# Narrow first row blocks in the products of quarters of a two-layer decoder

## The chip, the cores and the metric

The kernel runs on one core of a Trainium2 chip. The metric is the device time of one execution in microseconds (us); the time before is the median of three runs. The profile is one execution taken by the hardware profiler; its times are counted from the first instruction of the span.

Engine names: PE is TensorE (PEld its weight loads, which overlap the matmuls), DVE is VectorE, ACT is ScalarE, POOL is GpSimd, SP is SyncE, which here issues most DMAs. L1073 is line 1073 of the kernel.

## The reference

256 tokens of width 2048 pass through two layers, each a token mixer and a feed-forward part. Layer 0 mixes with forgetting attention, layer 1 with a mixture of dilated windows. The change lies in the feed-forward part:

```python
def rms_norm(x, g):
    xf = x.astype(jnp.float32)
    y = xf * lax.rsqrt(jnp.mean(xf * xf, axis=-1, keepdims=True) + EPS)
    return (y * g.astype(jnp.float32)).astype(x.dtype)

def sq_relu_mlp(h, w_up, w_down):
    a = jax.nn.relu(h @ w_up)
    return (a * a) @ w_down

for i in range(DEPTH):                      # DEPTH = 2
    h = rms_norm(x, mix_norm_g[i])
    ...                                     # mix: fox_attention or dilated_attention
    x = x + mix
    h = rms_norm(x, mlp_norm_g[i])
    x = x + sq_relu_mlp(h, mlp_w_up[i], mlp_w_down[i])
```

`w_up` is 2048 x 8192 and `w_down` 8192 x 2048, all in float32.

## The kernel before

**Products.** A float32 operand is split into a rounded high part and a residue, and a product is three matmuls: high by high, high by residue, residue by high. Weights stream from HBM in tiles of 256 rows by 512 columns (`raw`, five buffers, 512 KB each). ScalarE casts a tile to its high part (`wh`), VectorE subtracts to get the residue (`wl`); both have five buffers. `split` does this for one unit and is called each time TensorE has used one up, so the feeders run up to five units ahead of TensorE. An ordinary unit (a row block) takes twelve matmuls of 512 columns (L437 to L439).

**Products of quarters.** Of the feed-forward's up product, ten of sixteen column tiles in each layer, twenty in all, are computed with seven products of blocks in place of eight (a Strassen-like scheme, `SEVEN`): the 256 tokens are halved and the 256 x 512 weight tile is cut into four quarters of 128 rows by 256 columns. TensorE multiplies sums of the token halves (`sumT`, made once per layer) or the halves themselves (`hT`) with sums of quarters or the quarters themselves. Per weight tile two units come out of the feeders: `quarters` (three quarters of the tile as they are, 768 columns) and `sums` (four sums that VectorE forms in `sum_quarters`, 1024 columns). `slice_steps` then issues one slice: seven products of three matmuls. The slices are woven between the row blocks of other products at places listed by hand (`BETWEEN` and its sisters), eight slices for one column tile, so that a product of quarters has eight slices (`pr` 0 to 7) some 5 us apart. `halves_chain` afterwards combines the seven results on ScalarE and VectorE (L1038 to L1048).

**PSUM.** The seven results of a product, 128 x 256 each, lie in four banks of 512 columns: `SEVEN` lists for each its bank, the half of the bank, the weight quarter or sum, and the token operand:

```python
SEVEN = ((0, 0, 2, 5), (1, 0, 0, 4), (2, 0, 1, 0), (3, 0, 7, 6), (0, 1, 5, 3), (1, 1, 6, 2), (2, 1, 4, 1))
```

The first four products write the first halves of the four banks, the last three the second halves of banks 0 to 2. In the first slice of a product (`pr == 0`), the first matmul of each of products 0 to 2 streams 512 columns: its own weight quarter and, behind it, a quarter of zeros, which GpSimd writes into the free fourth quarter of that unit's `wh` (unit kind `"first quarters"`, L368). So the start of the accumulation group covers the whole bank, and the bank's second product only accumulates. All other matmuls of a slice stream 256 columns.

**Order.** The order of each engine's instructions is that of the trace of the Python program (`pin`). GpSimd's queue holds the zeroing, a few small vector operations and the accumulating DMAs that add the down product to the residual stream (`add_chain`, L945).

Of the kernel before, what the change touches and what calls it, by code (L numbers as in the profile page):

```python
# [9 lines left out]
F32 = mybir.dt.float32  # L10
# [11 lines left out]
NC = 512  # L22
NX = D // NC
KC = D // P
# [19 lines left out]
HC = NC // 2  # L44
# [61 lines left out]
def trunk(ctx: ExitStack, tc, x, fox_w_in, fox_b_f, fox_q_gain, fox_k_gain, fox_w_out, dil_w_in,  # L106
          dil_q_gain, dil_k_gain, dil_w_out, mix_norm_g, mlp_norm_g, mlp_w_up, mlp_w_down, out):
    nc = tc.nc
# [142 lines left out]
    plan = []  # L251

    units = []
    woven = {"count": 0, "due": {}, "do": None}

    def add(w, rows, cols):

        for r in range(rows[0], rows[1], RAW_SUB * P):
            units.append((len(plan), "rows"))
            plan.append((w, r, cols))  # L260
            for at in woven["due"].get(woven["count"], ()):
                units.extend(((len(plan), "quarters" if at[1] else "first quarters"), (len(plan), "sums")))
                plan.append(at)
            woven["count"] += 1

    def add_group(*chunks, parts=PARTS):

        for a, b in parts:
            for w, cols in chunks:
                add(w, (a * P, b * P), cols)  # L270

    def add_out(w):
        add_group(*((w, [(n * NC, NC)]) for n in range(3)), parts=OUT_PARTS)
        for n in range(3, NX):
            add(w, (0, D), [(n * NC, NC)])

    for j in range(4):
        for part in range(3):
            add(fox_w_in[0], (0, D), [(part * D + j * NC, NC)])
# [66 lines left out]
    def split(parts=(slice(0, W_SUB),)):  # L346
        i = state["split"]
        if i >= len(units):
            return
        hi = wpool.tile([P, W_SUB, NC], F32R, tag="wh", name=f"wh{i}", bufs=W_BUFS)  # L350
        lo = wpool.tile([P, W_SUB, NC], F32R, tag="wl", name=f"wl{i}", bufs=W_BUFS)
        splits.append((hi, lo))
        state["split"] += 1
        for part in parts:
            split_part(i, part)
        if parts:
            next_load()

    def split_part(i, part):
        nonlocal summing  # L360
        n, of = units[i]
        raw, (hi, lo) = raws[n], splits[i]
        if of == "sums":
            raw = quarters.pop()
        if "quarters" in of:

            if of == "first quarters":
                nc.gpsimd.memset(hi[:, 1, HC:NC].bitcast(F32), 0.0)  # L368
            flat_hi, flat_lo, flat = (x.rearrange("p k n -> p (k n)")[:, 0:3 * HC] for x in (hi, lo, raw))
            nc.scalar.copy(flat_hi, flat)  # L370
            for _ in summing or sum_quarters(n):
                pass
            summing = None
            nc.vector.tensor_sub(flat_lo, flat, flat_hi.bitcast(F32))  # L374
            return
        nc.scalar.copy(hi[:, part, :], raw[:, part, :])  # L376

        coming = i + 1 < len(units) and "quarters" in units[i + 1][1]
        if coming:
            summing = sum_quarters(units[i + 1][0])  # L380
            next(summing)
        nc.vector.tensor_sub(lo[:, part, :], raw[:, part, :], hi[:, part, :].bitcast(F32))  # L382
        if coming:
            next(summing)

    quarters, summing = [], None

    def sum_quarters(n):


        raw = raws[n]
        t = work.tile([P, 2, NC], F32, tag="sd", name=f"quarters{n}", bufs=1)
        neg, c, d = t[:, 0, HC:NC], t[:, 1, 0:HC], t[:, 1, HC:NC]
        nc.vector.tensor_sub(t[:, 0, :].rearrange("p (q n) -> p q n", q=2),
                             raw.rearrange("p k n -> p (k n)")[:, HC:3 * HC].rearrange("p (q n) -> p q n", q=2),
                             raw[:, 1, HC:NC].unsqueeze(1).to_broadcast([P, 2, HC]))
        yield
        nc.vector.tensor_add(c, raw[:, 0, HC:NC], neg)
        yield
        nc.vector.tensor_sub(d, raw[:, 0, 0:HC], c)  # L400
        quarters.append(t)
# [11 lines left out]
    def in_turn(w, apart=NC // 2):  # L413
        return w.rearrange("p (b h n) -> p b n h", n=apart, h=2)
# [644 lines left out]
    def slice_steps(tag, banks, pr):  # L1059

        (bh, bl), (th, tl) = splits[used[0]:used[0] + 2]
        for i, (bank, half, w, a) in enumerate(SEVEN):
            hi, lo = (in_turn((t if w > 3 else x)[:, w % 4 // 2, HC * (w % 2):HC * (w % 2) + HC], HC // 2)[:, 0]
                      for x, t in ((bh, th), (bl, tl)))
            if a < 4:
                ah, al = (x[:, a, :] for x in sumT[tag, pr])
            else:
                ah, al = (hT[tag][pr][:, a % 2, x, (a - 4) // 2 * P:((a - 4) // 2 + 1) * P] for x in range(2))
            to = banks[bank][:, HC * half:HC * half + HC]
            if pr == 0 and i < 3:  # L1070

                wide = bh.rearrange("p k (q n) -> p (k q) n", q=2)[:, w:4:3 - w]
                nc.tensor.matmul(banks[bank], ah, wide.rearrange("p b (h n) -> p b n h", h=2), start=True, stop=False)  # L1073
            else:
                nc.tensor.matmul(to, ah, hi, start=pr == 0 and i == 3, stop=False)  # L1075
            nc.tensor.matmul(to, ah, lo, start=False, stop=False)  # L1076
            nc.tensor.matmul(to, al, hi, start=False, stop=pr == KC // 2 - 1 and i > 2)  # L1077
            if i == 2 or i == 6:
                used[0] += 1
                split()  # L1080
                jobs.tick()

    def mlp(tag, **after):
# [3 lines left out]
        def one(b, n, pr):  # L1087
            if pr == 0:
                banks[:] = [pool.tile([P, NC], F32, tag=of, name=f"halves_{tag}_{b}_{n}_{i}")
                            for pool, of in ((ps_tp, "tp"), (ps_sc, "sc")) for i in range(2)]  # L1090
            jobs.need(("sums", tag, pr))
            slice_steps(tag, banks, pr)
            if pr == KC // 2 - 1:
                jobs.spawn(halves_chain(list(banks), f"{tag}a{b}", n, aTs[b], (tag, "free", b - 1, n),
                                        (tag, "halves") if (b, n) == (3, 3) else None))
# [28 lines left out]
    def normed(tag, col, wait=lambda n: 2, later=lambda n: 2):  # L1124
        ssp = norm_begin(tag)
        return lambda n: norm_chain(tag, col, n, ssp, wait(n), later(n))


    first = normed("n0", 0, lambda n: (0, 3, 5, 9)[n], lambda n: (13, 12, 9, 7)[n])
# [24 lines left out]
    row_blocks = [slice(i, i + 1) for i in range(W_SUB)]  # L1154
    split(())
    split_part(0, row_blocks[0])
    jobs.spawn(first(0))
    split_part(0, row_blocks[1])
    next_load()
    split(())  # L1160
# [85 lines left out]
```

## Time and profile before

| | |
|---|---|
| median of three runs | 2104.18 us (2104.1 to 2104.22) |
| profiled execution, first to last instruction | 2099.8 us, the only time given of it; the runs' median is 4.4 us more |
| TensorE (PE) busy | 2094.2 us, 11515 matmuls |
| VectorE (DVE) busy | 1775.9 us |
| ScalarE (ACT) busy | 1299.5 us |
| GpSimd (POOL) busy | 141.3 us |
| DMA | 518.28 MB, mean 247 GB/s |
| matmuls of the wide opening form (L1073) | 60 |
| GpSimd's zeroing (L368) | 20, 0.311 us each |

A row of the timeline gives the start in us, the duration in us, the engine, the line, the operation, the tile written and the tiles read, the shapes, and in brackets the idle time before it with what ended it. The recorded duration of a matmul includes the way through the array and overlaps the next matmul, so its cost in a stream is the distance between two starts. The waits name the waiting engine and line, what it waited for, the sum in us, the number of times and the longest. The chain is followed back from the last instruction; its pieces give a start, a length and an engine with its line.

### The profile page before, as it was taken

To read this page: it belongs to the slowest core of one execution; us is meant where nothing else is said; L and a number is where in the kernel's file an instruction comes from. 1 tells how busy PE (TensorE), PEld (TensorE's weight loads), DVE (VectorE), ACT (ScalarE), POOL (GpSimd) and SP (SyncE) were. 2 spreads that over 40 slices of the span, in tenths; PEclk is the share of its full clock that TensorE was granted. 3 is DMA by queue.
4 is the path that set the end of the run, shared out by engine and by line. 5 is a ranking of instruction groups with operands and counts; after the bars stand their busy time and mean duration, and the time that the engine had idled before them with its cause. 6 is when DMAs were issued, how large, how long until landed. Compare 5 with 4: busy or idle time off the path is not lost.

```text
span 2099.8 us, 32579 instructions
## 1 busy us (share of the span) xinstructions
PE 2094.2 (100%) x11515; PEld 1881.5 (90%) x11515; DVE 1775.9 (85%) x2613; ACT 1299.5 (62%) x1895; POOL 141.3 (7%) x162
## 2 busy tenths in 40 slices
PE   9999999999999999999999999999999999999999
PEld 7888888899999999998888888888899999999998
DVE  6888876989999999998768787767899989999974
ACT  6565654766666666664655665646656766666663
POOL 2000000001100100110010010000001101001000
PEclk9999999999999999999999999999999999999999
DMA  8888877887888877887877776867878878788884
GB/s 258 254 264 262 259 248 222 272 261 241 252 243 249 262 240 252 258 249 236 280 239 230 247 242 211 269 202 243 277 231 261 241 250 248 231 251 256 265 262 152
DMA packets 375010, 518.28 MB, mean 247 GB/s; under 512 B 43112, under 2 KB 176576, under 8 KB 374848
## 3 DMA queue, kind: packets, MB, share of 16 engines
q1 hardware_dynamic: 360608, 503.23, 75.4%
q0 software_dynamic: 13824, 12.59, 4.0%
q8 instruction: 90, 1.47, 0.3%
q14 instruction: 72, 0.59, 0.1%
q10 hardware_dynamic: 416, 0.39, 0.1%
HBM read 463.12 MB, written 40.39 MB: 240 GB/s over the span
## 4 chain that ended last, share of the span: by engine, by line
PE 100%; DVE 0%; ACT 0%; issue 0%
PE acc L437 26%; PE acc L438 26%; PE acc L439 26%; PE halves_n L1077 6%; PE halves_n L1076 6%; PE halves_n L1075 6%; PE halves_n L1073 1%; PE sc_d L749 0%; PE sc_f L749 0%; PE po_f L698 0%; PE po_d L698 0%; PE sc_d L746 0%; PE acc L486 0%; PE acc L485 0%; PE acc L487 0%; PE pf L760 0%
## 5 line engine op out<-in xcount | busy, mean ns | idle before, releaser
L382 DVE TENSOR_TENSOR wl<-raw,wh 128x1024 fp32r<-128x1024 f32 (+1 forms) x643 | 775.6, 1214 | 228.0 <-ACT wh L376 217.9
L376 ACT CAST wh<-raw 128x1024 fp32r<-128x1024 f32 (+1 forms) x643 | 664.9, 1043 | 403.7 <-PE acc L439 323.7
L437 PE MATMUL acc<-wh,hT_n 128*128 128x512 f32 x1280 | 486.5, 380 | 0.4 <-ACT hT_n L580 0.3
L438 PE MATMUL acc<-wl,hT_n 128*128 128x512 f32 x1280 | 485.4, 379 | 0.0
L439 PE MATMUL acc<-wh,hT_n 128*128 128x512 f32 x1280 | 485.3, 379 | 0.0
L376 ACT CAST wh<-quarters 128x1024 fp32r<-128x1024 f32 x160 | 168.0, 1050 | 260.8 <-DVE quarters L400 243.4
L439 PEld LDWEIGHTS acc<-wh,hT_n 128*128 128x128 f32 x1280 | 241.9, 189 | 34.6 <-DVE hT_n L581 0.4
L437 PEld LDWEIGHTS acc<-wh,hT_n 128*128 128x128 f32 x1280 | 242.1, 189 | 33.2 <-ACT hT_n L580 1.0
L438 PEld LDWEIGHTS acc<-wl,hT_n 128*128 128x128 f32 x1280 | 242.2, 189 | 32.6 <-DVE wl L382 0.5
L382 DVE TENSOR_TENSOR wl<-quarters,wh 128x1024 fp32r<-128x1024 f32 x160 | 195.1, 1219 | 43.0 <-ACT wh L376 43.0
L437 PE MATMUL acc<-wh,aTh_n1a 128*128 128x512 f32 x512 | 194.3, 379 | 0.0
L438 PE MATMUL acc<-wl,aTh_n1a 128*128 128x512 f32 x512 | 194.0, 379 | 0.0
L439 PE MATMUL acc<-wh,aTl_n1a 128*128 128x512 f32 x512 | 194.0, 379 | 0.0
L438 PE MATMUL acc<-wl,aTh_n3a 128*128 128x512 f32 x480 | 182.2, 380 | 0.0
L437 PE MATMUL acc<-wh,aTh_n3a 128*128 128x512 f32 x480 | 182.1, 379 | 0.0
L439 PE MATMUL acc<-wh,aTl_n3a 128*128 128x512 f32 x480 | 181.9, 379 | 0.0
L1077 PE MATMUL halves_n<-wh,sums_n 128*128 128x256 f32 x640 | 176.0, 275 | 0.0
L1076 PE MATMUL halves_n<-wl,sums_n 128*128 128x256 f32 x640 | 176.0, 275 | 0.0
L1075 PE MATMUL halves_n<-wh,sums_n 128*128 128x256 f32 x620 | 170.5, 275 | 0.0
L374 DVE TENSOR_TENSOR wl<-raw,wh 128x768 fp32r<-128x768 f32 x160 | 152.3, 952 | 0.0
L370 ACT CAST wh<-raw 128x768 fp32r<-128x768 f32 x160 | 133.1, 832 | 28.9 <-PE acc L439 15.1
L1077 PE MATMUL halves_n<-wh,hT_n 128*128 128x256 f32 x480 | 132.0, 275 | 0.0
(660 smaller groups left out, 3499.1 us busy)
## 6 DMA issues: line engine op xcount, KB each, us to landing
raw<-in_mlp_w_up_dram SPq DMA_DIRECT2D x256, 512.0 KB, 5.1
raw<-in_mlp_w_down_dram SPq DMA_DIRECT2D x256, 512.0 KB, 4.9
raw<-in_dil_w_in_dram SPq DMA_DIRECT2D x192, 256.0 KB, 3.5
raw<-in_fox_w_in_dram SPq DMA_DIRECT2D x94, 512.0 KB, 4.8
raw<-in_fox_w_out_dram SPq DMA_DIRECT2D x32, 512.0 KB, 4.9
raw<-in_dil_w_in_dram SPq DMA_DIRECT2D x32, 512.0 KB, 4.4
raw<-in_dil_w_out_dram SPq DMA_DIRECT2D x32, 512.0 KB, 3.6
x<-y_n POOLq DMA_DIRECT2D x96, 128.0 KB, 6.0
```

The costliest lines, as they stand in the source:

```text
L370: nc.scalar.copy(flat_hi, flat)
L374: nc.vector.tensor_sub(flat_lo, flat, flat_hi.bitcast(F32))
L376: nc.scalar.copy(hi[:, part, :], raw[:, part, :])
L382: nc.vector.tensor_sub(lo[:, part, :], raw[:, part, :], hi[:, part, :].bitcast(F32))
L437: nc.tensor.matmul(acc[t], ah[:, tok], hi, start=first, stop=False)
L438: nc.tensor.matmul(acc[t], ah[:, tok], lo, start=False, stop=False)
L439: nc.tensor.matmul(acc[t], al[:, tok], hi, start=False, stop=last)
L1073: nc.tensor.matmul(banks[bank], ah, wide.rearrange("p b (h n) -> p b n h", h=2), start=True, stop=False)
L1075: nc.tensor.matmul(to, ah, hi, start=pr == 0 and i == 3, stop=False)
L1076: nc.tensor.matmul(to, ah, lo, start=False, stop=False)
L1077: nc.tensor.matmul(to, al, hi, start=False, stop=pr == KC // 2 - 1 and i > 2)
```

## The change

The two kinds of first unit become one: GpSimd writes no zeros any more. In every slice all 21 matmuls stream 256 columns. In the first slice the bank's first product (half 0) opens the accumulation group; the first matmul of the bank's second product (half 1) opens none and falls on columns that nothing has been written to since that opening. `skip_group_check` concerns the program's own bookkeeping of groups and no instruction.

```diff
@@ add
             for at in woven["due"].get(woven["count"], ()):
-                units.extend(((len(plan), "quarters" if at[1] else "first quarters"), (len(plan), "sums")))
+                units.extend(((len(plan), "quarters"), (len(plan), "sums")))
                 plan.append(at)
@@ split_part
-        if "quarters" in of:
-
-            if of == "first quarters":
-                nc.gpsimd.memset(hi[:, 1, HC:NC].bitcast(F32), 0.0)
+        if of == "quarters":
             flat_hi, flat_lo, flat = (x.rearrange("p k n -> p (k n)")[:, 0:3 * HC] for x in (hi, lo, raw))
...
-        coming = i + 1 < len(units) and "quarters" in units[i + 1][1]
+        coming = i + 1 < len(units) and units[i + 1][1] == "quarters"
@@ slice_steps
             to = banks[bank][:, HC * half:HC * half + HC]
-            if pr == 0 and i < 3:
-
-                wide = bh.rearrange("p k (q n) -> p (k q) n", q=2)[:, w:4:3 - w]
-                nc.tensor.matmul(banks[bank], ah, wide.rearrange("p b (h n) -> p b n h", h=2), start=True, stop=False)
-            else:
-                nc.tensor.matmul(to, ah, hi, start=pr == 0 and i == 3, stop=False)
-            nc.tensor.matmul(to, ah, lo, start=False, stop=False)
-            nc.tensor.matmul(to, al, hi, start=False, stop=pr == KC // 2 - 1 and i > 2)
+            nc.tensor.matmul(to, ah, hi, start=pr == 0 and not half, stop=False, skip_group_check=True)
+            nc.tensor.matmul(to, ah, lo, start=False, stop=False, skip_group_check=True)
+            nc.tensor.matmul(to, al, hi, start=False, stop=pr == KC // 2 - 1, skip_group_check=True)
```

## The prediction

> **What bounds the kernel now.** I read the page's first and fourth parts, then TensorE's timeline inside the second half of the feed-forward layers, then the waits of the engines that feed TensorE.
>
> ```profile
> PE 2094.2 (100%) x11515; PEld 1881.5 (90%) x11515; DVE 1775.9 (85%) x2613; ACT 1299.5 (62%) x1895; POOL 141.3 (7%) x162
> ...
> PE 100%; DVE 0%; ACT 0%; issue 0%
> ```
>
> and the view of the cores, span and granted clock:
>
> ```profile
> core 0: 2099.8 us, clock 1.000
> ```
>
> TensorE is busy all the time, the chain that ended last runs through it alone, and its granted clock is full. A record of a matmul overlaps the next one, so a full PE row proves little by itself. What decides is the distance from one start to the next. The timeline of the first row block of a product of quarters (a slice of 21 matmuls, the first of its product):
>
> ```profile
> 450.61 0.38 PE L1073 MATMUL halves_n<-wh,hT_n 128*128 128x512 f32 x1
> 450.83 0.27 PE L1076 MATMUL halves_n<-wl,hT_n 128*128 128x256 f32 x1
> 450.94 0.28 PE L1077 MATMUL halves_n<-wh,hT_n 128*128 128x256 f32 x1
> ...
> 451.93 0.28 PE L1075 MATMUL halves_n<-wh,hT_n 128*128 128x256 f32 x1
> 452.04 0.28 PE L1076 MATMUL halves_n<-wl,hT_n 128*128 128x256 f32 x1
> ...
> 453.27 0.38 PE L437 MATMUL acc<-wh,aTh_n1a 128*128 128x512 f32 x1
> ```
>
> and the slice that follows in the same product:
>
> ```profile
> 455.86 0.27 PE L1075 MATMUL halves_n<-wh,hT_n 128*128 128x256 f32 x1
> ...
> 458.20 0.38 PE L437 MATMUL acc<-wh,aTh_n1a 128*128 128x512 f32 x1
> ```
>
> A wide matmul holds TensorE for 0.22 us (450.61 to 450.83), a narrow one for 0.11. The first slice takes 453.27 - 450.61 = 2.66 us, the ordinary one 458.20 - 455.86 = 2.34 us; 2.66 is 3 wide and 18 narrow spacings, 2.34 is 21 narrow ones. So nothing but the streaming of columns sets the time here: TensorE is not waiting for anybody.
>
> **The change part by part.** First, the three wide matmuls of each first slice become narrow.
>
> ```profile
> L1075 PEld LDWEIGHTS halves_n<-wh,sums_n x620: 192/192/192, 452.2 to 2022.6; 128*128 128x128 f32 x155
> ...
> L1073 PE MATMUL halves_n<-wh,hT_n x40: 379/380/454, 450.6 to 1978.5; 128*128 128x512 f32 x40
> ...
> L1073 PE MATMUL halves_n<-wh,sums_n x20: 382/382/402, 451.5 to 1978.9; 128*128 128x512 f32 x20
> ```
>
> These are rows of the view of the tile that the quarters' products write (count, then shortest, median and longest in ns). There are 40 + 20 = 60 of them, three for each of 20 products. The whole slices give the price with the least rounding: 2.66 - 2.34 = 0.32 us, and the single slices read 0.31 to 0.32; I take 0.314, which is 3 x 0.105. Twenty times that is 6.28 us.
>
> What no row of before shows is a matmul that neither accumulates nor starts a group, which the first matmuls of the banks' second products become (three in each first slice). I bound it from the rows on both sides: the accumulating narrow matmul at 0.11 (450.83 to 450.94), and, above, the wide one at 0.22. The nearest row is the fourth product's start at 451.93: it opens a group with 256 columns, so it overwrites, and the next one starts 0.11 later. I take 0.11, no extra cost. Something cheaper than 0.11 is excluded, since the same 256 columns stream in every case. The Trainium skill, "PSUM — Partial Sum Buffer", in its passage on two groups open in one bank, says that a start clears the written marks of the whole bank and that a later product on other columns then overwrites without a start; no run here shows that yet.
>
> The Trainium skill, "TensorE: Matmul & The Clock Gate", section "Back-to-back issue gap", has a rule that speaks against the gain: in a stream of weight load and matmul pairs the two share the spacing, about 81 ns at 128 columns and 131 ns at 512. By a straight line between these, an estimate, 256 columns would take 98 ns and the 60 edits would bring 60 x 0.033 = 2.0 us; the rows above (0.22 and 0.11) disagree, and the sum goes by them.
>
> Second, GpSimd's zeroing goes, 20 times.
>
> ```profile
> L368 POOL MEMSET wh<- x20: 311/311/312, 440.5 to 1969.2; 128x256 f32 x20
> ```
>
> and from the waits of the whole span (engine and line, released by, us in total, times, longest):
>
> ```profile
> POOL x L945 <- ACT y_n L944: 373.0, 23, 36.9
> ```
>
> The first one runs at 440.5, ten microseconds ahead of its slice at 450.61, and GpSimd is 7% busy. Behind it on GpSimd's queue stand the accumulating DMAs of L945, and what these waited for, 23 times and 373 us, is ScalarE's output, not the memset. So nobody gets work earlier: I cost it at nothing, and it needs no cover, as the work goes and isn't moved. The waits for a free bank, which now may stand before up to seven openings of a first slice instead of four, hold up everything behind them on TensorE if they are late; that is priced below.
>
> Third, whether the feeders keep up with a TensorE that is 0.314 us faster in 20 places. The same view of the waits holds this row:
>
> ```profile
> ACT wh L376 <- PE acc L439: 331.2, 240, 2.1
> ```
>
> ScalarE, the first of the two feeders, waited 240 times for TensorE to give a weight buffer back: at those points the feeders are as far ahead as five buffers allow, and a faster TensorE pulls them along. Between them they are on their own, and inside a product they are slower than TensorE. VectorE's timeline, one round of a row block and a slice:
>
> ```profile
> 1747.75 0.69 DVE L394 TENSOR_TENSOR quarters<-raw 128x512 f32<-128x512 f32 x1
> 1748.36 1.22 DVE L382 TENSOR_TENSOR wl<-raw,wh 128x1024 fp32r<-128x1024 f32 x1
> ...
> 1751.56 1.23 DVE L382 TENSOR_TENSOR wl<-quarters,wh 128x1024 fp32r<-128x1024 f32 x1 [0.32 <-ACT wh L376]
> 1752.82 0.69 DVE L394 TENSOR_TENSOR quarters<-raw 128x512 f32<-128x512 f32 x1
> ```
>
> A round takes VectorE 1752.82 - 1747.75 = 5.07 us; TensorE needs twelve wide matmuls (12 x 0.2155 = 2.59) and a slice (2.34), 4.93 us. Each round eats 0.14 us of the lead. The chain between 1700 and 2000 us, its longest pieces, shows where the lead was used up:
>
> ```profile
> 1749.77 0.35 PE acc L438
> 1754.84 0.35 PE acc L438
> 1759.91 0.35 PE acc L438
> 1780.49 0.32 PE halves_n L1073
> 1781.04 0.24 PE halves_n L1073
> 1860.47 0.24 PE acc L438
> ```
>
> Against 0.2155 these matmuls are late by 0.135 three times, then 0.10, 0.02 and 0.02: 0.55 us in all. So in two products of the second layer (the ones whose slices surround 1750 and 1860) VectorE sets the time, and TensorE's 0.314 us become waiting: 2 x 0.31 = 0.62 lost. The other products have room. Of those the tightest is the one ending in the slice at 678.55 (VectorE's row first, then TensorE's, with a slice of the round shown above):
>
> ```profile
> 677.44 1.23 DVE L382 TENSOR_TENSOR wl<-quarters,wh 128x1024 fp32r<-128x1024 f32 x1 [0.32 <-ACT wh L376]
> ```
>
> ```profile
> 678.55 0.27 PE L1075 MATMUL halves_n<-wh,hT_n 128*128 128x256 f32 x1
> ...
> 1752.11 0.27 PE L1075 MATMUL halves_n<-wh,hT_n 128*128 128x256 f32 x1
> ```
>
> The residues written by 678.67 are first read by the slice's eleventh matmul, 678.55 + 10 x 0.111 = 679.66: 0.99 us ahead. In the round without room above, the same operation ends at 1752.79 for a read at 1753.22: 0.43 ahead. The room is 0.56 us, more than the 0.314 that one first slice takes from it, and the buffers refill between products.
>
> The stop at 1780 is of another kind, a bank that the product before has not given back:
>
> ```profile
> 1779.80 0.41 DVE L1045 TENSOR_TENSOR c_n3a<-c_n3a,halves_n 128x256 f32<-128x256 f32 x1
> 1780.25 0.42 DVE L1047 TENSOR_TENSOR c_n3a<-halves_n,c_n3a 128x256 f32<-128x256 f32 x1
> ```
>
> VectorE reads the old sums of a bank until 1780.21 and those of another until 1780.67, and the late pieces at 1780.49 and 1781.04 are the openings of the second and third wide product, some 0.3 us behind these ends. These readers run on VectorE's time, so the second and third openings can't come earlier than now, and only what is saved in the third remains: 0.105 of 0.314, 0.21 lost. The sum: 6.28 - 0.62 - 0.21 = 5.45 us. The span of 2099.8 becomes 2094.3; the runs' median of 2104.18 lies 4.4 us above the span, and nothing of that start and end is touched, so 2104.18 - 5.45 = 2098.7 us.
>
> **The rivals.** (a) The narrow opening isn't shorter: its 0.19 us weight load (the LDWEIGHTS row) sets the spacing, or a start takes the time of the whole bank that it clears. With the load, 60 x (0.2155 - 0.19) = 1.5 us, so 2102.7; with the bank, nothing, 2104.2. For it speaks that loads are as busy as 90% of the span; against it the narrow start at 451.93 with its neighbour 0.11 later, and the ordinary slice, where 21 loads went by in 2.34 us. The shared spacing of the skill's TensorE page would end at about the same place. Chance 0.06.
>
> (b) The feeders take back more. If the room in the five next tightest products were under 0.31 too, 5 x 0.314 = 1.57 us more would be lost: 2100.3, which is no measurable change. For it speaks that VectorE's round is longer than TensorE's everywhere in these products; against it the 0.56 us of room in the tightest one. Chance 0.05.
>
> (c) Slower: a matmul that overwrites unwritten columns without a start lets the matmul before it leave the array. A narrow record lasts 0.275 and its successor starts after 0.11, so emptying costs 0.164 each. For the 60 second openings that is 9.8 us: 2098.7 + 9.8 = 2108.5; if all 120 openings that become narrow did it, 2118. It decides from 0.161 us for each of the 60, since 5.45 + 4.2 must be made up. No row has such a matmul, which leaves it open; against it the 0.11 after the narrow start, an overwrite too. Chance 0.04.
>
> **How the numbers follow.** The measurement can tell about 0.2%, 4.2 us: faster is under 2099.97, slower over 2108.39. My own case has 0.85. Its low end is nothing lost and the present 0.55 us of stops gone as well: 2104.18 - 6.28 - 0.55 = 2097.3. The high end is the lower edge of (b) with the spread of the three runs, 2100.4. This leaves out (a), (c) and a part of (b), so no wider range is called for. Faster 0.85, the same 0.11 from (a) and (b), slower 0.04.
>
> **What would show it.** All matmuls of the quarters have 256 columns, 60 more on the line that holds the first of the three products, and L368's memset is gone from GpSimd. First slices last 2.34 us like the others. The pieces near 1750 and 1860, some 4 us earlier then, are longer by 0.31 us in sum for each of the two products, and the stop at the first slice after the former grows to about 0.33 us. The first layer, ten products, is shorter by 3.1 us with no stop in it. I am wrong if a second opening in a bank is followed by more than 0.11 us, if stops appear in the first layer, or if TensorE waits for banks in other first slices.

## The result, and the profile after

The changed kernel takes 2097.78 us (median of six runs, 2095.8 to 2098.54) against 2104.14 us of before (six runs, 2103.01 to 2105.31). The ratio is 0.9971, 95% interval 0.996 to 0.9982: 6.4 us less by the medians. The forecast was 2098.7, between 2097.3 and 2100.4.

The page of after, its span and the engines' busy times:

```profile
span 2096.7 us, 32543 instructions
...
PE 2089.2 (100%) x11515; PEld 1877.3 (90%) x11515; DVE 1774.4 (85%) x2613; ACT 1296.4 (62%) x1895; POOL 134.8 (6%) x142
```

The count of matmuls is the same, GpSimd has its 20 instructions less, and the span is only 3.1 us shorter. The six runs after list span and time for each execution, and the time is 1.7 us above the span every time. By that distance the profiled execution of before, with its 2099.8, would have taken 2101.5: it was a lucky one, some 2.6 us under its median. (Later runs of the kernel before list both too, with the same 1.7 us.) So a single pair of profiles doesn't show the size of the gain; its parts do.

TensorE's timeline at the first slice of a product, where before had three wide matmuls:

```profile
451.47 0.27 PE L1067 MATMUL halves_n<-wh,hT_n 128*128 128x256 f32 x1
451.58 0.28 PE L1068 MATMUL halves_n<-wl,hT_n 128*128 128x256 f32 x1
...
452.81 0.28 PE L1067 MATMUL halves_n<-wh,sums_n 128*128 128x256 f32 x1
452.92 0.28 PE L1068 MATMUL halves_n<-wl,sums_n 128*128 128x256 f32 x1
...
453.14 0.28 PE L1067 MATMUL halves_n<-wh,sums_n 128*128 128x256 f32 x1
453.25 0.28 PE L1068 MATMUL halves_n<-wl,sums_n 128*128 128x256 f32 x1
...
453.81 0.38 PE L434 MATMUL acc<-wh,aTh_n1a 128*128 128x512 f32 x1
```

The slice takes 453.81 - 451.47 = 2.34 us; before it was 2.66. The row at 451.47 opens a bank with 256 columns, the rows at 452.81 and 453.14 are second products on unwritten columns without a group of their own: each of the three is followed after 0.11 us.

What the feeders take back is seen in TensorE's late starts. Two places of after, the first in VectorE's and TensorE's timelines of the first layer:

```profile
672.44 1.23 DVE L379 TENSOR_TENSOR wl<-quarters,wh 128x1024 fp32r<-128x1024 f32 x1 [0.32 <-ACT wh L373]
```

```profile
672.99 0.27 PE L1067 MATMUL halves_n<-wh,hT_n 128*128 128x256 f32 x1
```

The residues end at 673.67 and are first read at 672.99 + 1.11 = 674.10: 0.43 us ahead, which is no room, in the sixth slice of the product for which the prediction counted 0.99 in the seventh. The second place is the first slice at 1776.8 in the second layer, VectorE's rows and then TensorE's:

```profile
1768.30 1.23 DVE L379 TENSOR_TENSOR wl<-raw,wh 128x1024 fp32r<-128x1024 f32 x1 [1.24 <-ACT wh L373]
...
1778.10 0.41 DVE L1042 TENSOR_TENSOR c_n3a<-c_n3a,halves_n 128x256 f32<-128x256 f32 x1
```

```profile
1777.04 0.28 PE L1069 MATMUL halves_n<-wh,hT_n 128*128 128x256 f32 x1
1778.65 0.35 PE L1067 MATMUL halves_n<-wh,hT_n 128*128 128x256 f32 x1 [1.34 <-DVE c_n3a L1042]
```

TensorE stands for 1.5 us until the product before has been read out of a bank. VectorE reads late; it stood for 1.24 us itself at 1768.30, and ScalarE's row just ahead of that shows what it stood for, a weight tile that landed late:

```profile
1767.22 2.19 ACT L373 CAST wh<-raw 128x1024 fp32r<-128x1024 f32 x2 [1.59 <-DMA raw<-in_mlp_w_down_dram]
```

The same kind of stop, 0.19 us long in all, stands in the first slice at 695.70 in the first layer, VectorE's reads and then the openings some 0.15 us behind their ends:

```profile
695.46 0.41 DVE L1042 TENSOR_TENSOR c_n1a<-c_n1a,halves_n 128x256 f32<-128x256 f32 x1
695.91 0.42 DVE L1044 TENSOR_TENSOR c_n1a<-halves_n,c_n1a 128x256 f32<-128x256 f32 x1
```

```profile
696.03 0.34 PE L1067 MATMUL halves_n<-wh,hT_n 128*128 128x256 f32 x1
...
696.48 0.35 PE L1067 MATMUL halves_n<-wh,sums_n 128*128 128x256 f32 x1
```

The two later profiles of this kernel have it there too, with 0.23 and 0.19 us.

### The profile page after: what moved, and what is told of

It reads as the page before. It is cut to its first block, busy times and chain, and to the rows that moved or that the text cites. A ratio compares the mean times of both kernels' runs of the same rounds, so it can differ in the third digit from the quotient of the medians.

```text
span 2096.7 us, 32543 instructions
## 1 busy us (share of the span) xinstructions
PE 2089.2 (100%) x11515; PEld 1877.3 (90%) x11515; DVE 1774.4 (85%) x2613; ACT 1296.4 (62%) x1895; POOL 134.8 (6%) x142
## 4 chain that ended last, share of the span: by engine, by line
PE 95%; DVE 2%; DMA 1%; issue 1%; ACT 0%; SPq 0%; ACTq 0%; DVEq 0%
PE acc L434 25%; PE acc L435 25%; PE acc L436 25%; PE halves_n L1069 6%; PE halves_n L1068 6%; PE halves_n L1067 6%; DVE wl L379 1%; DMA raw<-in_mlp_w_up_dram 1%; ACT wh L373 0%; PE sc_d L746 0%; DMA x<-in_x_dram 0%; PE sc_f L746 0%; PE po_d L695 0%; PE sc_d L743 0%; PE acc L482 0%
## 5 line engine op out<-in xcount | busy, mean ns | idle before, releaser
L435 PE MATMUL acc<-wl,hT_n 128*128 128x512 f32 x1280 | 485.4, 379 | 0.0
L436 PE MATMUL acc<-wh,hT_n 128*128 128x512 f32 x1280 | 485.3, 379 | 0.0
L1067 PE MATMUL halves_n<-wh,sums_n 128*128 128x256 f32 x640 | 176.2, 275 | 0.0
L1069 PE MATMUL halves_n<-wh,sums_n 128*128 128x256 f32 x640 | 176.0, 275 | 0.0
L942 POOL DMA_DIRECT2D x<-y_n x96 | 84.2, 1357 | 970.3 <-ACT y_n L941 837.1
```

Of the source, the lines that this page charges most:

```text
L435: nc.tensor.matmul(acc[t], ah[:, tok], lo, start=False, stop=False)
L436: nc.tensor.matmul(acc[t], al[:, tok], hi, start=False, stop=last)
L942: nc.gpsimd.dma_start(xt[n][:, t, h * HC:h * HC + HC], y, accum_op=ALU.add)
L1067: nc.tensor.matmul(to, ah, hi, start=pr == 0 and not half, stop=False, skip_group_check=True)
```

## The experiments

All ten were timed beside the kernel before. For each profile I also took, from TensorE's timeline, the distance from the first to the last start of the quarters' matmuls in each layer, and the stops in it (how much later than 0.2155 or 0.111 us after its predecessor a matmul starts, where that is over 0.025). The stretch between the layers' slices is 594.83 or 594.84 us, and the stretch behind the last one 76.8 to 76.9, in all of these profiles but that of the GpSimd sum (77.2 behind); the stretch ahead of the first varies from 450.6 to 452.4 without a pattern.

| kernel | ratio to before (95%) | layer 1: us, stops | layer 2: us, stops |
|---|---|---|---|
| before | 1 | 488.46, 0.00 | 489.01, 0.52 |
| after | 0.9971 (0.996 to 0.9982) | 485.73, 0.40 | 487.79, 2.48 |
| after, in the second group of runs | 0.9976 (0.9965 to 0.9987) | 486.18, 0.84 | 486.55, 1.22 |
| after, in the fourth group | 0.9972 (0.9961 to 0.9983) | 486.54, 1.19 | 486.05, 0.70 |
| zeroing put back | 0.9975 (0.9965 to 0.9985) | 485.55, 0.19 | 487.48, 2.17 |
| narrow in layer 1 only | 0.9987 (0.9978 to 0.9996) | 486.72, 1.40 | 488.82, 0.37 |
| narrow in layer 2 only | 0.9988 (0.9979 to 0.9997) | 489.32, 0.85 | 486.83, 1.51 |
| wide in two slices | 1.0025 (1.0015 to 1.0035) | 491.58, 0.00 | 493.12, 1.53 |
| after, lighter sums | 0.9964 (0.9952 to 0.9977) | 485.33, 0.00 | 485.33, 0.00 |
| before, lighter sums | 0.9993 (0.9984 to 1.0002) | 488.46, 0.00 | 489.08, 0.62 |
| slices spread | 0.9982 (0.9974 to 0.9991) | 487.65, 2.33 | 487.97, 2.65 |
| pause moved | 0.998 (0.9971 to 0.9989) | 486.55, 1.20 | 486.70, 1.36 |
| sums first | 1.0005 (0.9996 to 1.0014) | 488.56, 3.25 | 490.34, 5.03 |
| sum on GpSimd | 1.0473 (1.0459 to 1.0487) | 538.51, 53.32 | 538.56, 53.39 |

Less its stops, every layer comes to 485.2 to 485.4 us where it is narrow, to 488.5 where it is wide and to 491.6 with the wide form in two slices. So the streaming and the stops are all that differs between these layers.

Theory A was that the gain is the streaming of 60 matmuls and that VectorE, with the banks it must read, takes a part back.

**The zeroing put back.** The change without its second part:

```diff
+            if n in firsts:
+                nc.gpsimd.memset(hi[:, 1, HC:NC].bitcast(F32), 0.0)
             nc.scalar.copy(flat_hi, flat)
```

> The changed kernel with GpSimd's 20 zeroings put back (their values are read by nobody now). Theory A, the gain is the narrower streaming of 60 matmuls alone: the time is that of the changed kernel within 0.3%, about 2097.8 us, ratio to before 0.997, and first slices of 2.34 us. Rival B, part of the gain comes from the zeroing that is gone: the time goes back towards before by up to 20 x 0.31 = 6.2 us, to 2104.

2097.56 us, ratio 0.9975: that of the changed kernel. Its GpSimd groups hold the 20 zeroings again:

```profile
L371 POOL MEMSET wh<- 128x256 f32 x20 | 6.2, 312 | 574.0 <-PE halves_n L1074 259.6 <-DVE wl L384 229.6 <-PE acc L441 84.8
```

So their 6.2 us of GpSimd cost nothing that the timed runs, good to some 2 us, or the layers less their stops can tell, and rival B falls.

**Narrow in one layer only.** From the kernel before, with `NARROW` 0 for the first and 1 for the second:

```diff
-            if pr == 0 and i < 3:
+            narrow = tag == ("n1", "n3")[NARROW]
+            if pr == 0 and i < 3 and not narrow:
```

> Narrow openings in the ten products of the first layer only; the second layer as before. Theory A: 30 x 0.105 = 3.1 us saved, less what stops near VectorE's limit take (up to 0.5), so 2101.3 us and the distance from the first to the last slice of layer 1 shorter by 2.7 to 3.1 us, that of layer 2 unchanged. Rival C, the gain is the whole span's mood (DMA timing) and not the openings: no difference between the layers.

> Narrow openings in the ten products of the second layer only. Theory A: 3.1 us saved in streaming, 0.6 to 0.8 taken back by the products in which VectorE sets the time, and up to 1.5 more if a late weight tile delays the bank readers, as in the profile after: between 0.9 and 2.5 us saved, 2101.6 to 2103.2 us; layer 1 unchanged. Rival C as above: no difference between the layers.

2100.72 and 2099.99 us; by the ratios 2.7 and 2.5 us saved. The layer that is narrow is shorter, the other isn't, and without their stops the narrow ones are at 485.3 and the wide ones at 488.5: the place of the gain is shown, and rival C falls. The even split was not expected: the second layer gave 2.5, at the upper end of what I allowed. In the profile of the first of these two runs the narrow layer is 1.74 us shorter and not 2.7 to 3.1, as it had 1.40 us of stops where at most 0.5 was allowed. And the first layer of the second run, which stayed wide, had 0.85 us of stops where before's profile had none: stops in the first layer are not the narrow form's alone.

**Twice as many wide matmuls.**

```diff
-            if pr == 0 and i < 3:
+            if pr < 2 and i < 3:
...
-                nc.tensor.matmul(banks[bank], ah, wide.rearrange("p b (h n) -> p b n h", h=2), start=True, stop=False)
+                nc.tensor.matmul(banks[bank], ah, wide.rearrange("p b (h n) -> p b n h", h=2), start=pr == 0, stop=False)
```

GpSimd writes the zeros for the second slices too.

> The kernel before with the wide form in the first two slices of each product (120 wide matmuls, 40 zeroings; adding zeros). Theory A, a dose: 60 x 0.105 = 6.3 us more streaming, less 0.3 to 0.6 where TensorE now waits less for VectorE and the banks: 2109.8 to 2110.4 us, and second slices of 2.65 us. Rival B, streaming is hidden beside the feeders: 2104 to 2106 us.

2107.68 us, ratio 1.0025, which is 5.3 us more; layer 1, without a stop, is 491.58 - 488.46 = 3.12 us longer for 30 more wide matmuls, 0.104 each. The dose holds per layer. The total lies under the 2109.8 to 2110.4 expected, mostly because the kernel before took 2102.74 in this group and not 2104.

**Lighter sums on VectorE.** Two operations of 256 columns become one of 512; the fourth sum is left out, and a copy of the third stands in its place:

```diff
-        nc.vector.tensor_add(c, raw[:, 0, HC:NC], neg)
+        nc.vector.tensor_add(t[:, 1, :].rearrange("p (q n) -> p q n", q=2),
+                             raw[:, 0, HC:NC].unsqueeze(1).to_broadcast([P, 2, HC]),
+                             neg.unsqueeze(1).to_broadcast([P, 2, HC]))
         yield
-        nc.vector.tensor_sub(d, raw[:, 0, 0:HC], c)
```

> The changed kernel with VectorE's last two operations on the sums of quarters made one of 512 columns; the fourth sum is left out (a copy of the third stands in its place). VectorE's round falls from 5.07 us to about 4.85, below TensorE's 4.93. Theory A, the stops that take back part of the gain are VectorE's: they fall from 2.0 to 2.6 us (both layers) to under 0.4, and the profiled distance from first to last slice is 485.3 to 485.6 in each layer, about 2 us less than the changed kernel in all. Rival D, the stops come from late weight tiles whatever VectorE does: 1 to 2.5 us of stops remain.

> The kernel before with the same lighter sums (the fourth left out). Theory A: its wide openings remain, its stops of about 0.5 us go; 0.3 to 1 us under before, and 6.2 us above the changed kernel with the lighter sums, the whole price of 60 x 0.105 with nothing taken back. Rival D: the distance between the two is no larger than between the changed kernel and before, 5 to 5.5 us.

A round in VectorE's timeline, of the changed kernel with the lighter sums:

```profile
1744.00 0.69 DVE L391 TENSOR_TENSOR quarters<-raw 128x512 f32<-128x512 f32 x1
1744.61 1.22 DVE L379 TENSOR_TENSOR wl<-raw,wh 128x1024 fp32r<-128x1024 f32 x1
1745.74 0.68 DVE L395 TENSOR_TENSOR quarters<-raw,quarters 128x512 f32<-128x512 f32 x1
...
1748.87 0.69 DVE L391 TENSOR_TENSOR quarters<-raw 128x512 f32<-128x512 f32 x1
```

1748.87 - 1744.00 = 4.87 us, under TensorE's 4.93, and both layers run without one stop: 485.33 each. 488.46 - 485.33 = 3.13 us for 30 matmuls is the bare price, 6.26 for both layers. The two kernels stand at 2096.09 and 2101.89 us, 5.8 apart; by their ratios 6.1. In both kernels the small stops that come once a round are gone. Near 1750, near 670 or in both places, they stand in each of the eight profiles that have the full sums and VectorE's order and slices as they were: those are VectorE's, as theory A says.

But the kernel before with lighter sums keeps a stop of 0.62 us behind 1854.6, and rival D has its part. ScalarE's rows, of this kernel and then of the changed one with lighter sums, at the same work:

```profile
1850.08 0.62 ACT L1026 CAST aTh_n3a<-turned_n3a 128x512 fp32r<-128x512 f32 x1 [4.13 <-DMA turned_n3a<-blocks_n3a]
```

```profile
1843.10 0.62 ACT L1023 CAST aTh_n3a<-turned_n3a 128x512 fp32r<-128x512 f32 x1 [0.69 <-DMA turned_n3a<-blocks_n3a]
```

ScalarE waits here for a DMA that brings activations back transposed, and the weight casts stand behind it in its queue. Over the twelve profiles without the sum on GpSimd and the new order of VectorE, the same wait was 0.53, 0.54, 0.69, 1.50, 1.65, 1.83 and 2.75 us with no stop of TensorE in this product, and 2.86, 3.08, 3.42, 3.61 and 4.13 us with 0.46, 1.22, 1.02, 1.22 and 0.62 us of stops, the first of them 3 to 5 us later. So the transfers that came latest go with stops, the latest of them in spite of the lighter sums (the 0.62), and the run without a single stop was also one in which nothing came late there.

**Other places for the slices.** Three slices, a pause, five slices, the first and the last a row block earlier:

```diff
-BETWEEN = (..., 7, 8, 9, 10, 11, 12, 13, 15, ...)
+BETWEEN = (..., 6, 7, 8, 10, 11, 12, 13, 14, ...)
-LAST_BETWEEN = (..., 3, 4, 5, 6, 7, 8, 9, 11, ...)
+LAST_BETWEEN = (..., 2, 3, 4, 6, 7, 8, 9, 10, ...)
```

> The changed kernel with the slices of two products placed otherwise: a pause of one row block after the third slice, and the last slice one row block earlier, so that VectorE catches up and the banks' readers have one row block more. Theory A: the stops at 1736 to 1757, 1777 and 1851 to 1857 go, 1 to 2 us less than the changed kernel. Rival D: stops of 1 to 2 us remain somewhere, and the time is that of the changed kernel.

2099.44 us, ratio 0.9982, and 5.0 us of stops in the profiled execution, which at 2101.35 us is the slowest of the eleven: a miss. The first slice now comes one row block nearer to the product before it, and TensorE meets that product's readers in the bank (its timeline):

```profile
647.68 0.35 PE L1067 MATMUL halves_n<-wh,hT_n 128*128 128x256 f32 x1 [0.74 <-DVE c_n1a L1042]
```

The second attempt left the first and last slice where they were:

```diff
-BETWEEN = (..., 7, 8, 9, 10, 11, 12, 13, 15, ...)
+BETWEEN = (..., 7, 8, 9, 10, 12, 13, 14, 15, ...)
-LAST_BETWEEN = (..., 3, 4, 5, 6, 7, 8, 9, 11, ...)
+LAST_BETWEEN = (..., 3, 4, 5, 6, 8, 9, 10, 11, ...)
```

> The changed kernel with the pause of the two longest runs of slices moved from before their last slice to after their fourth; first and last slice where they were. Theory A: the lead that VectorE loses, 0.14 us a round, is refilled halfway, so the stops inside the runs (1736 to 1757, 1851 to 1857) go, but the banks' readers find VectorE less far ahead at the end: 0 to 1.5 us under the changed kernel, with what stops are left at the next first slice. Rival D: the same stops in the same places, no difference.

The stops behind the first slices shrink to 0.20 us, and 2.4 us of them stand in first slices, the most 1.03 in the one at 1926.36 and 0.61 in the one at 695.34. The profiled execution took 2097.75 us; the median is 2099.12, ratio 0.998: the places moved as theory A said, but the time did not fall.

**The fourth sum on GpSimd.**

```diff
-        nc.vector.tensor_sub(d, raw[:, 0, 0:HC], c)
+        nc.gpsimd.tensor_sub(d, raw[:, 0, 0:HC], c)
```

> The changed kernel with the fourth sum of quarters made by GpSimd in place of VectorE; nothing left out. Theory A: VectorE's round falls by one start distance of 0.34 us to about 4.75, below TensorE's 4.93, and the stops go as in the kernel with lighter sums: about 485.3 us in each layer, 2096 us, 2 us under the changed kernel. Rival E: GpSimd is too slow or its queue is held (the accumulating DMAs of L942 take 3.5 us to issue four and wait for ScalarE), sums come late, TensorE stops for them: 2099 to 2110 us.

2202.59 us, ratio 1.0473: far off theory A and beyond rival E's range too, but on its side. The sum takes GpSimd 1.3 us and stands between VectorE's third sum and the cast in the chain sum, cast, residue; the groups of GpSimd and ScalarE show it, with 409.8 us in which the cast waited for GpSimd:

```profile
L397 POOL TENSOR_TENSOR quarters<-raw,quarters 128x256 f32<-128x256 f32 x160 | 207.7, 1298 | 856.6 <-DVE quarters L395 541.6 <-issue 141.1 <-ACT y_n L941 59.1
...
L373 ACT CAST wh<-quarters 128x1024 fp32r<-128x1024 f32 x160 | 167.3, 1046 | 423.7 <-POOL quarters L397 409.8 <-PE halves_n L1069 10.0 <-PE acc L436 3.7
```

**VectorE's order.** The sums all ahead of the row block's residue:

```diff
-            next(summing)
+            for _ in summing:
+                pass
         nc.vector.tensor_sub(lo[:, part, :], raw[:, part, :], hi[:, part, :].bitcast(F32))
-        if coming:
-            next(summing)
```

> The changed kernel with VectorE's order changed, nothing added or left out: the three sums of quarters stand together ahead of the row block's residue, so that ScalarE's cast of the sums runs while VectorE works and the 0.32 us for which VectorE waits in each round go. Theory A: the round falls from 5.07 us to 4.75, below TensorE's 4.93, the stops of the rounds go, and what can remain is a bank's late reader: 485.3 to 486.0 us in each layer, 2096 to 2097 us. Rival F: the row block's residue, which now comes 0.8 us later and was the one that stopped TensorE, stops it more: 2099 us or above.

2104.42 us, ratio 1.0005: the whole gain gone. VectorE's round did fall to 1746.87 - 1742.09 = 4.78 us, but the row block's residue starts 0.9 us later in it (1.52 us behind the first sum where it was 0.61). VectorE's and TensorE's rows:

```profile
1742.09 1.22 DVE L380 TENSOR_TENSOR wl<-raw,wh 128x1024 fp32r<-128x1024 f32 x1
...
1746.87 1.22 DVE L380 TENSOR_TENSOR wl<-raw,wh 128x1024 fp32r<-128x1024 f32 x1
```

```profile
1737.40 0.48 PE L434 MATMUL acc<-wl,aTh_n3a 128*128 128x512 f32 x1 [0.77 <-DVE wl L380]
```

The first rounds of a product, in which VectorE also turns the squares of the product before, now stop TensorE for 0.9 us each. Rival F was right: the rate of a round isn't enough, the operation that is needed first has to come first.

**The changed kernel again,** beside the second and the fourth group:

> The changed kernel again, beside the three others on the same chip. Theory A: layer distances of 485.3 us plus its stops, which come out between 0.3 and 2.6 us, and 4.5 to 6 us under before; rival D the same.

> The changed kernel once more, beside the reordered one on the same chip. Theory A: 485.3 us in each layer plus its stops, some 0.3 to 2.5 us of them, 1 to 2 us above the reordered kernel. Rival F: at or under the reordered kernel.

2098.14 and 2097.2 us. The stops of three executions of one kernel, 2.88, 2.06 and 1.89 us, are for the most part in other places each time. Of the kernels that leave nothing out, none beats the changed one.

## Why the prediction was right, and where it was off

**The streaming, right.** 60 times 0.105 = 6.28 us was forecast; two layers without stops differ by 2 x 3.13 = 6.26.

**The opening on unwritten columns, right.** The nearest row, 0.11, was the price; rival (c) needed 0.16 more for each, rival (a) 0.19 or 0.22 for the spacing. The trace of after decides against both: its rows have 0.111 us and 0.2155, and the 60 edits brought 6.26. The Trainium skill, "TensorE: Matmul & The Clock Gate", section "Back-to-back issue gap", would by the line through its two sustained figures, an estimate, give 98 ns against 131 at 512 columns and 2.0 us in all; this case's trace does not agree. The Trainium skill, "PSUM — Partial Sum Buffer", says of two groups in a bank that the second overwrites where a start has cleared the marks; the runs agree, with 60 such openings in each execution.

**The zeroing at nothing, right,** by the run with it put back.

**What is taken back, right in kind and off in size.** VectorE's round of 5.07 us and the small stops it makes are shown by the lighter sums, which end them; the larger stops go with transfers that land late, which the prediction did not have. But 0.83 us, with two products and one bank, was read from one execution of before, and four statements fell with that. "The room is 0.56 us" held for one execution only: in after the same product started with less lead (3.71 us in its first slice, 4.51 before) and had 0.43 us ahead where 0.99 had been, no room at all. "The first layer ... with no stop in it" was wrong, with 0.40 to 1.19 us in the three profiles of after. The stop at the first slice after 1750 came to 1.7 us instead of 0.33 in the first profile, and to nothing and 0.18 in the two later ones. And TensorE did wait for a bank in another first slice, the 0.2 us near 696 in all three; the prediction had named both as signs that it was wrong. Nor did the two products behave alike: the one around 1750 went from 0.41 us of stops to 0.78, 0.00 and 0.51, the one around 1860 from nothing to 0.00, 1.22 and 0.00, where 0.31 more had been counted for each.

The narrow kernel (after three times, and the one with the zeroing) lost 1.89 to 2.88 us to stops; 0.52 stood in the one profile of before. The layers that stayed wide in the runs with one narrow layer give the wide form a second draw each, 0.85 in the first layer and 0.37 in the second. By these few draws a narrow first layer loses 0.80 us on average (five profiles) against 0.43 (two), a narrow second 1.62 against 0.45: some 1.5 us is taken back, an estimate, where 0.83 was forecast; that is part of the way to rival (b).

**The baseline, off.** "The runs' median lies 4.4 us above the span" took a difference between two executions for a fixed start and end, which are 1.7 us. The two errors work against each other: the kernel before has its slower executions too, so less is lost net than its lucky profile suggests. How large its stops are on average wasn't measured beyond those draws. By the timed ratios the net gain is 5.0 to 6.1 us; 5.45 was forecast. So the 6.28 of the sum is a hit by its mechanism, and that what was subtracted brought the total so close is in part luck.

That late transfers set off the larger stops is read from twelve traces at one place, in the order of the waits, and from five at the other: there the weight tile was waited for 1.59, 1.13 and 1.01 us (after, narrow in layer 2 only, the zeroing put back) and the next first slice had 1.71, 1.25 and 1.27 us of stops, while in the two later profiles of after no tile was waited for and the stops were nothing and 0.18. No run made a transfer earlier or later, so it is not shown by an experiment, and why they land late stays open.

## What to carry to other kernels

In a stretch where the starts on TensorE follow each other without a gap, an edit to its stream is worth the spacing, and that is counted from starts, not from recorded durations. Then ask of the engine that feeds it whether its round is longer or shorter than TensorE's, and treat the lead that one profile shows as one draw: executions differ by more than a 0.3 us edit uses up. A feeder that is short by 0.14 us in a round is mended by giving it less work (here a sum was left out, so no usable kernel shows it); moving its operations about, or onto a slower engine in the same chain, cost more here than it saved.

## What the runs showed of the hardware

The wait for one and the same transfer lay between 0.53 and 4.13 us in twelve profiles, with nearly the same work around it. A subtraction of 128 x 256 took GpSimd 1.30 us on average (0.72 to 2.04) where VectorE's took 0.42, three times as long, and 53 us of stops per layer came with 80 of them in the chain. A matmul of 256 columns that overwrites without opening a group costs the same 0.11 us as one that accumulates.
